# Spreading 512 token factors over all partitions: a store and a load in place of diagonals and a matmul, and the shift added one step later

## The chip, the cores and the metric

One core of a Trainium2 chip runs the kernel. The metric is the device time of one execution in microseconds; a comparison goes by the median of several executions. TensorE is called PE here (PEld its weight loads), VectorE DVE, ScalarE ACT, and SyncE SP, which issues every DMA of this kernel.

## The reference

One layer of a streaming encoder, 1024 tokens of width 2048, float32. A modulated RMSNorm is followed by one wide projection, two groups of heads, gates, an output projection, a residual and a last norm:

```
shift, scale, gate = split(silu(c) @ w_ada + b_ada, 3)
hn   = rmsnorm(x, norm_w) * (1 + scale) + shift          # the change is here
proj = hn @ w_in                                          # 2048 x 7184
a_out = differential attention (8 heads, rope, chunk mask), normed, gated
b_out = gated linear attention (4 heads, chunks of 64), normed, gated
out  = rmsnorm(x + gate * (concat(a_out, b_out) @ w_out), final_norm_w)
```

Per token t and channel k, hn[t,k] = x[t,k] * r[t] * a[k] + s[k], with r[t] the reciprocal root mean square of the token, a = norm_w * (1 + scale) and s = shift.

## The kernel before, in words

The tokens are worked in two halves of 512. In each half `hn` lies in SBUF transposed, as 16 tiles of 128 channels by 512 tokens. Every matrix is split into two parts, `hi` (rounded to the matmul's format) and `lo` (the rest), and each product is three matmuls, hi*hi, hi*lo, lo*hi. Weights come through `wload`: a DMA on SP into one of two `wr` buffers (L177), a rounding copy on ScalarE (L179), a subtraction on VectorE (L180), into one of three `w` buffers. `proj_b` (L190 to L192) and `proj_a` (L218 to L220) are the projections and fill most of PE's time.

A half goes through four groups g (`unit`), each with two attention heads and one head of gated linear attention. The attention of a head makes scores in one of two PSUM banks (`s`, L665, L666), takes their maximum on VectorE (L669, scaled at L673), the exponential on ScalarE (L678), then transposes (`tp`, L708) and multiplies with the values (`av`, L720 to L722). Small PSUM tiles of all stages (`tp`, `av`, the norms' sums, `o` and others) share the two banks of the pool `ms_p`.

`hn` of the second half is prepared while the first half runs, in small pieces of side work. The list `later` holds them, and `wload` takes one out after every second weight load (after two of three in the second half). The piece is traced behind ScalarE's rounding copy (`issue_after(paced.ins)`), which orders its ScalarE instructions alone; its VectorE instructions and DMAs have no such order. The tile framework's scheduler then lays out every engine's order from a timeline that it simulates, by priority in program order, and every engine and the DMA queue of SP work in that order. All side work goes through `stage`, two buffers of 128x512, which take turns:

- 16 pieces load x in token layout and square it with a sum on ScalarE (L932).
- `end` turns the sums into the 512 factors `r`, 128 partitions by 4 (`ssq[:, 20:24]`, L937 and `rsqrt_small`). They are needed along the free dimension on all partitions: four diagonals (L942), a matmul with ones into a bank of `ms_p` (L944), and a copy to `rb` (L945).
- 16 pieces load x transposed, multiply by `a_c` and `rb` (L949), add `s_c` (L950) and store the result in DRAM (`hn_d`, L951).

At the end of the first half, `second_hn` loads two channel tiles at a time back (`xtb`, L963) and splits them into the `hn` tiles as PE is done with the old ones: L229 (copy on ScalarE) and L230 (subtraction on VectorE), by the helper `split`. The first half does the same job by `activations`, with the shift added inside the split (L322, L323).

Behind the 16 pieces, `later` is filled with the rows of the adaLN gate (`gate_rows`, L918, L920, L912), 16 loads and multiply-adds per quarter; their accumulator `gacc` shares its buffer with `rb`.

Of the kernel before, what the change touches and what calls it, by code (L numbers as in the profile page):

```python
# [10 lines left out]
F32 = mybir.dt.float32  # L11
F32R = mybir.dt.float32r
BF16 = mybir.dt.bfloat16
AF = mybir.ActivationFunctionType
ALU = mybir.AluOpType
# [4 lines left out]
P = 128  # L20
# [3 lines left out]
TOK = 512  # L24
# [71 lines left out]
def body(ctx, tc, A, out):  # L96
    nc = tc.nc
    tc.keep_in_program_order(nc.scalar.preload_act_table_set("natural_log_exp_and_others"))
    V, G, SC, PE = nc.vector, nc.gpsimd, nc.scalar, nc.tensor
# [8 lines left out]
    misc = ctx.enter_context(tc.tile_pool(name="misc", bufs=1))  # L108
    pj_p = ctx.enter_context(tc.tile_pool(name="pj", bufs=4, space=PSUM))
    sc_p = ctx.enter_context(tc.tile_pool(name="sc", bufs=2, space=PSUM))  # L110
    ms_p = ctx.enter_context(tc.tile_pool(name="ms", bufs=2, space=PSUM))
    dram = ctx.enter_context(tc.tile_pool(name="dram", bufs=1, space=DRAM))
# [3 lines left out]
    vs_d = [dram.tile([P, 4, 2, P], F32, name=f"vsd{h}", tag=f"vsd{h}") for h in range(HEADS)]  # L116
    s_d = [dram.tile([P, 256], F32, name=f"sd{g}", tag=f"sd{g}") for g in range(GHEADS)]
    gate_d = dram.tile([1, D], F32, name="gate_d")
    hn_d = [dram.tile([P, 2, TOK], F32, name=f"hnd{k}", tag=f"hnd{k}") for k in range(KT // 2)]


    ident = const.tile([P, P], F32, name="ident")
# [3 lines left out]
    ones_f = ones.bitcast(F32)  # L126
# [11 lines left out]
    s_c = const.tile([P, KT], F32, name="s_c")  # L138
# [13 lines left out]
    def rsqrt_small(dst, src, n, scale):  # L152
        t = small()
        m = small()
        V.tensor_scalar(m[:, :n], src, scale, EPS, ALU.mult, ALU.add)
        SC.activation(t[:, :n], m[:, :n], AF.Ln)
        SC.activation(t[:, :n], t[:, :n], AF.Exp, scale=-0.5)
        V.tensor_mul(m[:, :n], m[:, :n], t[:, :n])
        V.tensor_mul(m[:, :n], m[:, :n], t[:, :n])
        V.tensor_scalar(m[:, :n], m[:, :n], -0.5, 1.5, ALU.mult, ALU.add)  # L160
        V.tensor_mul(dst, m[:, :n], t[:, :n])
# [25 lines left out]
    hn = [None] * KT  # L187
# [40 lines left out]
    def split(hi, lo, src, lo_eng=None):  # L228
        SC.copy(hi, src)  # L229
        (lo_eng or V).tensor_tensor(lo, src, hi.bitcast(F32), ALU.subtract)  # L230
# [36 lines left out]
    with tc.high_priority():  # L267
# [12 lines left out]
        m, r, t = rsb[:, 0, :], rsb[:, 1, :], acc_p.tile([P, TOK], F32, name="nt", tag="pt", bufs=6)  # L280
# [540 lines left out]
    def unit(half, g, first, kdec):  # L821
# [52 lines left out]
        if swap:  # L874
            second_hn()
# [52 lines left out]
    def norm_rows():  # L928
        ssq = const.tile([P, 24], F32, name="ssq_b")

        def sq(i, raw):
            SC.activation(raw, raw, AF.Square, accum_out=ssq[:, i:i + 1])  # L932
            if i == 15:
                end()

        def end():
            V.tensor_reduce(ssq[:, 16:20], ssq[:, 0:16].rearrange("p (t q) -> p t q", q=4), AX.X, ALU.add)  # L937
            rsqrt_small(ssq[:, 20:24], ssq[:, 16:20], 4, 1.0 / D)
            dg = misc.tile([P, 2, TOK], F32, name="rdiag", tag="rt", bufs=2)[:, 0, :]
            r_ = misc.tile([P, TOK], F32, name="rb", tag="gacc")  # L940
            for t_ in range(4):
                V.tensor_scalar(dg[:, t_ * P:(t_ + 1) * P], ident, ssq[:, 20 + t_:21 + t_], None, ALU.mult)  # L942
            ps_ = ms_p.tile([P, TOK], F32, name="rb_ps", tag="ms")
            PE.matmul(ps_, ones_f, dg, start=True, stop=True)  # L944
            SC.copy(r_, ps_)  # L945
            rb.append(r_)

        def act(kt, u):
            V.scalar_tensor_tensor(u, u, a_c[:, kt:kt + 1], rb[0], ALU.mult, ALU.mult)  # L949
            V.tensor_scalar_add(u, u, s_c[:, kt:kt + 1])  # L950
            nc.sync.dma_start(hn_d[kt // 2][:, kt % 2, :], u)  # L951

        x_row = lambda i: A["x"][TOK + i // 4 * P:TOK + (i // 4 + 1) * P, i % 4 * 512:(i % 4 + 1) * 512]
        return ([(x_row(i), lambda raw, i=i: sq(i, raw)) for i in range(16)]
                + [(A["xt"][1][:, kt, :], lambda u, kt=kt: act(kt, u)) for kt in range(KT)])

    def second_hn():
        while later:
            later.pop(0)()
        for k0 in range(0, KT, 2):  # L960
            tag = ("ka", "va", "kb")[k0 // 2 % 3]
            r3 = hd_p.tile([P, 2, TOK], F32, name=f"xtb{k0}", tag=tag, bufs=2 if tag == "kb" else None)
            nc.sync.dma_start(r3, hn_d[k0 // 2])  # L963
            for kk in range(2):
                kt = k0 + kk
                hn[kt] = hn_p.tile([P, 2, TOK], F32R, name=f"hn{kt}", tag=f"hn{kt}")
                split(hn[kt][:, 0, :], hn[kt][:, 1, :], r3[:, kk, :], lo_eng=V)


    later += run_ahead(norm_rows())  # L970
# [36 lines left out]
    for half in range(2):  # L1007
# [6 lines left out]
        ssq = const.tile([P, 4, N_SSQ], F32, name=f"ossq{half}", tag="ossq", bufs=2)  # L1014
        tot = const.tile([P, 8], F32, name=f"otot{half}", tag="otot", bufs=2)
        oview = out[half * TOK:(half + 1) * TOK, :].rearrange("(t p) c -> p t c", p=P)
        for m in range(4):
# [26 lines left out]
            for k0 in range(0, KT, 2):  # L1044
                w = wload(A["wout"][m][:, k0:k0 + 2, :], 1024)
                for t_ in range(4):
                    for kk in range(2):
                        kt = k0 + kk
# [59 lines left out]
```

## Time and profile before

| | us |
|---|---|
| median of 3 executions | 1954.24 (1954.07 to 1956.40) |
| the profiled execution, its own time | 1955.52 |
| its span, first to last instruction | 1953.7 |
| PE busy | 1905.5 |
| DVE busy | 1321.9 |
| ACT busy | 968.7 |

The profile is of one execution, so times read in it are set against its 1955.52 us; its span leaves 1.8 us around the instructions. Matmuls are pipelined, so the duration of one overlaps the next; the distance between two starts is what a matmul takes. In the stretch view, busy time that equals the length of the stretch means that PE had no gap. A wait is put down to what released it last.

### The profile page before, as it was taken

The page shows a single profiled execution, that of the slowest core. Times are in us where ns is not written, and L with a number is a line of the kernel's source. Part 1 is how long each engine was busy: PE and PEld are TensorE (multiplying, and loading weights), DVE is VectorE, ACT ScalarE, POOL GpSimd, SP SyncE. Part 2 cuts the span into 40 slices and gives each one's busy share as a digit, 9 for nine tenths or more (in the row PEclk, how much of TensorE's full clock was granted, in tenths as well). Part 3 has the DMA queues.
Part 4 walks back from the last instruction along what each step waited for, and adds up shares of the span by engine and source line. Part 5 has one row for each costly group of instructions (what it writes and reads, how often), then busy time and mean ns, then how long its engine had stood idle before and what let it go on. Part 6 is the DMA issues. An engine that isn't in the chain of part 4 may idle for free.

```text
span 1953.7 us, 28965 instructions
## 1 busy us (share of the span) xinstructions
PE 1905.5 (98%) x11118; PEld 1677.0 (86%) x11118; DVE 1321.9 (68%) x2496; ACT 968.7 (50%) x1811; POOL 0.7 (0%) x6
## 2 busy tenths in 40 slices
PE   7999999999989999999999999999999999899998
PEld 4888999899868989889899898989888998688888
DVE  7897876577779767656676666866785675534444
ACT  4222865566545566545545555554654544323323
POOL 0000000000000000000000000000000000000000
PEclk9899999999999999999999999999999999799999
DMA  9884434332665444433344323533263723466543
GB/s 362 294 290 136 155 125 141 119 106 87 209 210 166 136 138 150 135 89 101 97 154 117 106 91 108 162 111 99 87 198 117 267 86 106 167 239 213 162 150 120
DMA packets 111758, 298.16 MB, mean 153 GB/s; under 512 B 11098, under 2 KB 31322, under 8 KB 111108
## 3 DMA queue, kind: packets, MB, share of 16 engines
q1 hardware_dynamic: 111620, 296.32, 46.6%
q8 instruction: 87, 1.43, 0.3%
q14 instruction: 51, 0.42, 0.1%
HBM read 258.00 MB, written 38.28 MB: 152 GB/s over the span
## 4 chain that ended last, share of the span: by engine, by line
PE 86%; DMA 6%; DVE 6%; issue 1%; ACT 1%; SPq 0%; DVEq 0%; ACTq 0%
PE pa L218 8%; PE pa L220 8%; PE pa L219 8%; PE pa L1051 4%; PE pa L1052 4%; PE pa L1053 4%; PE pb_dk L190 2%; PE pb_dk L191 2%; PE pb_dk L192 2%; PE pb_gg L190 2%; PE pb_dg L191 2%; PE pb_dq L192 2%; PE pb_dq L191 2%; PE pb_dq L190 2%; PE pb_dg L192 2%; PE pb_gg L192 2%
## 5 line engine op out<-in xcount | busy, mean ns | idle before, releaser
L180 DVE TENSOR_TENSOR w<-wr,w 128x1024 fp32r<-128x1024 f32 (+1 forms) x294 | 352.1, 1198 | 276.0 <-ACT w L179 274.8
L179 ACT CAST w<-wr 128x1024 fp32r<-128x1024 f32 (+1 forms) x294 | 303.2, 1031 | 431.2 <-PE pa L1053 116.1
L220 PE MATMUL pa<-w,hn 128*128 128x256 f32 (+1 forms) x1152 | 328.2, 285 | 0.0
L218 PE MATMUL pa<-w,hn 128*128 128x256 f32 (+1 forms) x1152 | 327.7, 285 | 0.0
L219 PE MATMUL pa<-w,hn 128*128 128x256 f32 (+1 forms) x1152 | 327.7, 285 | 0.0
L219 PEld LDWEIGHTS pa<-w,hn 128*128 128x128 f32 x1152 | 219.6, 191 | 2.4 <-issue 0.2
L218 PEld LDWEIGHTS pa<-w,hn 128*128 128x128 f32 x1152 | 219.5, 191 | 2.3 <-issue 0.5
L220 PEld LDWEIGHTS pa<-w,hn 128*128 128x128 f32 x1152 | 219.5, 191 | 1.5 <-issue 0.2
L678 ACT ACTIVATE p<-s,sm 128x512 f32<-128x512 f32 (+2 forms) x192 | 110.7, 580 | 130.1 <-DVE sm L675 59.0
L1051 PE MATMUL pa<-w,mx 128*128 128x512 f32 x384 | 150.7, 392 | 0.4 <-DVE h L996 0.4
L1052 PE MATMUL pa<-w,mx 128*128 128x512 f32 x384 | 150.4, 392 | 0.0
L1053 PE MATMUL pa<-w,mx 128*128 128x512 f32 x384 | 149.9, 392 | 0.0
L669 DVE TENSOR_REDUCE sm<-s 128x1 f32<-128x512 f32 (+2 forms) x192 | 105.5, 551 | 46.7 <-PE s L666 44.1
L190 PE MATMUL pb_gg<-hn,w 128*128 128x512 f32 x224 | 88.1, 394 | 0.6 <-DVE vb L230 0.6
L191 PE MATMUL pb_dk<-hn,w 128*128 128x512 f32 x224 | 88.1, 393 | 0.0
L190 PE MATMUL pb_dk<-hn,w 128*128 128x512 f32 x224 | 88.1, 393 | 0.0
L190 PE MATMUL pb_dg<-hn,w 128*128 128x512 f32 x224 | 88.1, 393 | 0.0
L191 PE MATMUL pb_gg<-hn,w 128*128 128x512 f32 x224 | 88.0, 393 | 0.0
L192 PE MATMUL pb_dq<-hn,w 128*128 128x512 f32 x224 | 87.9, 392 | 0.0
L191 PE MATMUL pb_dg<-hn,w 128*128 128x512 f32 x224 | 87.8, 392 | 0.0
L192 PE MATMUL pb_gg<-hn,w 128*128 128x512 f32 x224 | 87.8, 392 | 0.0
L192 PE MATMUL pb_dk<-hn,w 128*128 128x512 f32 x224 | 87.6, 391 | 0.0
(394 smaller groups left out, 4376.9 us busy)
## 6 DMA issues: line engine op xcount, KB each, us to landing
wr<-in_winb SPq DMA_DIRECT2D x142, 512.0 KB, 3.8
wr<-in_wina SPq DMA_DIRECT2D x72, 512.0 KB, 3.8
wr<-in_wout SPq DMA_DIRECT2D x64, 512.0 KB, 3.5
ada<-in_wada SPq DMA_DIRECT2D x44, 512.0 KB, 5.0
stage<-in_wgate SPq DMA_DIRECT2D x64, 256.0 KB, 3.0
mx<-mixd SPq DMA_DIRECT2D x32, 512.0 KB, 8.1
ada_kdec<-in_wada SPq DMA_DIRECT2D x20, 512.0 KB, 6.6
mixd<-wr_d SPq DMA_DIRECT2D x16, 512.0 KB, 4.5
```

Source lines behind the costliest of these rows:

```text
L179: paced = SC.copy(w[:, 0, :n], raw[:, :n])
L180: (lo_eng or V).tensor_tensor(w[:, 1, :n], raw[:, :n], w[:, 0, :n].bitcast(F32), ALU.subtract)
L190: PE.matmul(ps, w_hi, h[:, 0, :], start=first, stop=False)
L191: PE.matmul(ps, w_hi, h[:, 1, :], start=False, stop=False)
L192: PE.matmul(ps, w_lo, h[:, 0, :], start=False, stop=last)
L218: PE.matmul(o, ah, wh, start=st, stop=False, skip_group_check=True)
L219: PE.matmul(o, ah, wl, start=False, stop=False, skip_group_check=True)
L220: PE.matmul(o, al, wh, start=False, stop=kt == KT - 1, skip_group_check=True)
L678: SC.activation(p_[:, :n], pss[pi][:, :n], AF.Exp, bias=nm, scale=0.125, accum_out=sm[:, 4 + 2 * m_ + pi:5 + 2 * m_ + pi])
L1051: PE.matmul(pss[t_], ah, wh, start=kt == 0, stop=False)
L1052: PE.matmul(pss[t_], ah, wl, start=False, stop=False)
L1053: PE.matmul(pss[t_], al, wh, start=False, stop=kt == KT - 1)
```

## The change

The factors go from SBUF to a DRAM row `r_d` by one DMA and from there to all 128 partitions by another. The diagonals, the matmul and the copy go. The 16 transposed rows no longer add the shift before they are stored; it is added when the two parts are made, the high part by an activation with a bias, the low part by one instruction with two scalar steps.

```
+    r_d = dram.tile([1, TOK], F32, name="r_d")
...
         def end():
             V.tensor_reduce(ssq[:, 16:20], ssq[:, 0:16].rearrange("p (t q) -> p t q", q=4), AX.X, ALU.add)
             rsqrt_small(ssq[:, 20:24], ssq[:, 16:20], 4, 1.0 / D)
-            dg = misc.tile([P, 2, TOK], F32, name="rdiag", tag="rt", bufs=2)[:, 0, :]
             r_ = misc.tile([P, TOK], F32, name="rb", tag="gacc")
-            for t_ in range(4):
-                V.tensor_scalar(dg[:, t_ * P:(t_ + 1) * P], ident, ssq[:, 20 + t_:21 + t_], None, ALU.mult)
-            ps_ = ms_p.tile([P, TOK], F32, name="rb_ps", tag="ms")
-            PE.matmul(ps_, ones_f, dg, start=True, stop=True)
-            SC.copy(r_, ps_)
+            nc.sync.dma_start(r_d.rearrange("o (t p) -> (o p) t", p=P), ssq[:, 20:24])
+            nc.sync.dma_start(r_, r_d[0:1, :].to_broadcast([P, TOK]))
             rb.append(r_)
 
         def act(kt, u):
             V.scalar_tensor_tensor(u, u, a_c[:, kt:kt + 1], rb[0], ALU.mult, ALU.mult)
-            V.tensor_scalar_add(u, u, s_c[:, kt:kt + 1])
             nc.sync.dma_start(hn_d[kt // 2][:, kt % 2, :], u)
...
                 hn[kt] = hn_p.tile([P, 2, TOK], F32R, name=f"hn{kt}", tag=f"hn{kt}")
-                split(hn[kt][:, 0, :], hn[kt][:, 1, :], r3[:, kk, :], lo_eng=V)
+                hi, lo, shift = hn[kt][:, 0, :], hn[kt][:, 1, :], s_c[:, kt:kt + 1]
+                SC.activation(hi, r3[:, kk, :], AF.Identity, bias=shift)
+                V.scalar_tensor_tensor(lo, r3[:, kk, :], shift, hi.bitcast(F32), ALU.add, ALU.subtract)
```

## Rows read from the trace of the kernel before

**Rows 1.** The page: busy us (share of the span) and instructions of each engine.

```profile
PE 1905.5 (98%) x11118; PEld 1677.0 (86%) x11118; DVE 1321.9 (68%) x2496; ACT 968.7 (50%) x1811; POOL 0.7 (0%) x6
```

**Rows 2.** Stretches: from:to, length, busy us per engine, clock, DMA share, GB/s.

```profile
506.00:545.00 39.00, 39.00 (x176) 32.34 (x175) 31.32 (x54) 21.02 (x38) 0.00 (x0) 1.00 0.69 227
545.00:575.00 30.00, 26.30 (x119) 19.95 (x117) 23.19 (x63) 13.09 (x29) 0.00 (x0) 1.00 0.67 209
575.00:610.00 35.00, 30.17 (x233) 28.49 (x232) 28.86 (x70) 18.10 (x38) 0.00 (x0) 1.00 0.63 194
...
759.00:784.00 25.00, 25.00 (x190) 24.08 (x189) 22.47 (x34) 15.75 (x26) 0.00 (x0) 1.00 0.53 173
```

**Rows 3.** Waits of PE, 545 to 610 us: total us, times, longest.

```profile
PE s L665 <- ACT p L678: 4.6, 5, 1.9
```

**Rows 4.** Waits of DVE, 545 to 610 us.

```profile
DVE stage L949 <- DMA stage<-in_xt: 6.8, 7, 3.1
DVE gacc L920 <- DMA stage<-in_wgate: 4.1, 5, 1.3
DVE gacc L918 <- DMA stage<-in_wgate: 1.8, 1, 1.8
```

**Rows 5.** Waits of DVE, 506 to 545 us.

```profile
DVE stage L949 <- DMA stage<-in_xt: 7.3, 4, 4.4
```

**Rows 6.** Timeline of PE around 504 us: start, us, instruction.

```profile
504.40 1.02 PE L944 MATMUL rb_ps<-rdiag,ones 128*128 128x512 f32 x2
...
505.49 0.39 PE L192 MATMUL pb_dk<-hn,w 128*128 128x512 f32 x1
```

**Rows 7.** Tile `ssq_b`: the instruction that finishes the factors.

```profile
L161 DVE TENSOR_TENSOR ssq_b<-sm,sm x1: 164/164/164, 462.1 to 462.1; 128x4 f32<-128x4 f32 x1
```

**Rows 8.** Tile `stage`: ns min/median/max, first and last start us.

```profile
L949 DVE SCALAR_TENSOR_TENSOR stage<-stage,a_c,rb x16: 744/752/755, 506.1 to 573.3; 128x512 f32<-128x512 f32 x16
L950 DVE TENSOR_SCALAR stage<-stage,s_c x16: 406/480/487, 508.0 to 574.6; 128x512 f32<-128x512 f32 x16
...
L918 DVE TENSOR_SCALAR gacc<-stage,vec x4: 475/483/486, 578.2 to 1415.5; 128x512 f32<-128x512 f32 x4
...
L912 DVE TENSOR_TENSOR gacc<-gacc,stage x4: 672/673/680, 617.4 to 1455.1; 1x512 f32<-1x512 f32 x4
```

**Rows 9.** The page: DMA issues, KB each, median us from issue to landing.

```profile
wr<-in_winb SPq DMA_DIRECT2D x142, 512.0 KB, 3.8
...
ind<-in_ind SPq DMA_DIRECT2D x1, 1.0 KB, 9.1
```

**Rows 10.** Line L951, the 16 stores of rows to DRAM.

```profile
DMA to landing us min/median/max: 2.0/2.5/5.0
```

**Rows 11.** Tile `gate_d`: its loads from one DRAM row to all partitions.

```profile
DMA to landing us min/median/max: 3.1/4.6/7.8
```

**Rows 12.** Tile `xtb`: the split of the second half.

```profile
L229 ACT CAST hn<-xtb x16: 602/616/620, 759.7 to 780.6; 128x512 fp32r<-128x512 f32 x16
L230 DVE TENSOR_TENSOR hn<-xtb,hn x16: 682/684/693, 760.4 to 782.9; 128x512 fp32r<-128x512 f32 x16
```

**Rows 13.** Line L322, the high part with bias in the first half.

```profile
L322 ACT ACTIVATE hn<-xt,s_c x16: 720/725/728, 25.8 to 174.2; 128x512 fp32r<-128x512 f32 x16
```

**Rows 14.** Line L323, the low part with the shift in the first half.

```profile
L323 DVE SCALAR_TENSOR_TENSOR hn<-xt,s_c,hn x16: 739/746/753, 26.7 to 176.5; 128x512 fp32r<-128x512 f32 x16
```

**Rows 15.** Timeline, 468 to 478 us: a weight load and a cast.

```profile
468.30 0.33 SPq L177 DMA_DIRECT2D wr<-in_wina  x1
...
477.55 1.05 ACT L179 CAST w<-wr 128x1024 fp32r<-128x1024 f32 x1 [1.73 <-PE pa L220]
```

**Rows 16.** Timeline, 779 to 791 us: the last split, the first users.

```profile
779.01 0.40 PE L190 MATMUL pb_dk<-hn,w 128*128 128x512 f32 x1
...
782.94 0.68 DVE L230 TENSOR_TENSOR hn<-xtb,hn 128x512 fp32r<-128x512 f32 x1
...
790.45 0.39 PE L192 MATMUL pb_dk<-hn,w 128*128 128x512 f32 x1
```

## The prediction

> **What bounds the kernel now.** I read the page first. PE is busy 1905.5 of 1953.7 us [rows 1], so a change pays only if it takes work off PE or fills one of PE's gaps, 48.2 us in all. The stretch view then shows where gaps stand near this change: none from 506 to 545 us (39.00 of 39.00), 3.70 us from 545 to 575 and 4.83 us from 575 to 610, 8.53 us together [rows 2]. The clock is 1.00 in all of them, so they are waits, not a slower PE. PE's waits in 545 to 610 name the cause: the largest is a score matmul (L665) waiting for ScalarE's exponential (L678), which frees its PSUM bank [rows 3]; that waits for VectorE's maximum. VectorE in turn stands, in the same stretch, 6.8 us for the x rows of the side work (L949) and 4.1 + 1.8 us for the gate rows that follow (L920, L918), 12.7 us in all [rows 4]. VectorE runs in order, so a side row whose load has not landed holds up the softmax behind it. PE loses 8.53 / 12.7 = 0.67 us for each us of such standing. But from 506 to 545, where PE has projections and the gated linear attention, VectorE stands 7.3 us for the same rows [rows 5] and PE loses nothing. The price of a side row thus depends on which stage it falls in.
>
> The last view is the time at which the factors come. They are finished on VectorE at 462.3 us (L161, 462.1 plus 0.16) [rows 7]. The matmul that spreads them runs only at 504.40 [rows 6], and the first of the 16 rows that use them at 506.1 [rows 8]. PE has no gap in between, the diagonals are made right behind L161, so what holds the matmul is its turn for one of the two banks of the `ms` pool, in which it stands in line with the heads' tiles. The 16 rows then run as fast as store, reload and arithmetic allow, 506.1 to 573.3, and the gate rows, which nothing paces on VectorE, follow from 578.2 to 617.4 [rows 8].
>
> **The change part by part.**
>
> *The matmul goes.* Between 504.40 and the start of L192 at 505.49 stand the two passes of the matmul and one L191 [rows 6]; L191 alone would take the 0.23 us by which such matmuls follow each other (48 of them, 779.01 to 790.45, with a few others between, give 0.24) [rows 16]. 1.09 - 0.23 = 0.86 us of a full PE come off. The four diagonals and the copy of `rb_ps` are on VectorE and ScalarE, in stretches where PE does not wait: nothing, and with that cover gone a bank and an `rt` buffer are free earlier, no loss.
>
> *Store and load.* Neither is in the trace. The store is 2 KB in 512 pieces of four bytes. Below, the fastest store of a row, 2.0 us; above, the `ind` load with its 128 pieces of eight bytes, 9.1 us, queued at the start of the kernel behind the first megabytes [rows 9, 10]. The load is like `gate_d` to all partitions: 3.1 to 7.8, median 4.6 [rows 11]. I take 2.5 (median of the row stores; the queue is light at 462 us) and 4.6, with two issues of 0.33 [rows 15]: the factors are in SBUF at 462.3 + 2.5 + 4.6 + 0.7 = 470.1. Bounds: 468.1 and 479.9. All of them lie before 506.1; the rows start 36 us earlier (26 to 38).
>
> *SP's queue.* The load waits on SP for the store. Behind it stand weight loads, the next at 468.30, whose cast runs at 477.55; with 3.8 us to land, 5.45 us are spare [rows 9, 15]. Holding SP from 462.6 to 465 costs nothing; even 9.1 us (to 472) use 3.7 of the 5.45.
>
> *VectorE's queue.* If the first row stands in VectorE's order before its factors have landed, the low parts of weights (L180) and attention's probabilities wait behind it, and PE for those. At most that is from about 463 to 479.9, 17 us; at least nothing. The planner simulates both DMAs too, so I take 1 us, at 0.67: +0.7.
>
> *The add goes from the rows.* 16 x 0.48 = 7.7 us of VectorE [rows 8]. Two buffers alternate, so the chain of rows loses 8 x 0.48 = 3.8 us. On PE it is nothing by itself: work that VectorE does while PE is full.
>
> *Side work moves.* The rows now end at 573.3 - 36.0 - 3.8 = 533.5, before the softmax stretch; the gate rows move from 578.2 to 538.4 and end at 577.6. So in 545 to 610 only the gate rows are left, in 32.6 us of it. They cost 4.83 us in 35 us [rows 2], 0.138 per us: 4.5. Of 8.53 us, 4.0 come back. Bounds: all 8.53 (the gate rows fall among projections, as the x rows did in 506 to 545), or none (a gate row costs there what both did).
>
> *Shift added at the split.* On ScalarE the cast of 0.616 us becomes an activation with bias, 0.725 as in the first half; on VectorE 0.684 becomes 0.746 [rows 12 to 14]: 16 x 0.11 = 1.7 us and 16 x 0.06 = 1.0 us. This is in 759 to 784, where PE is full and VectorE busy 22.47 of 25 us [rows 2]. The last low part starts at 782.94; its first user is among the last matmuls of `pb_dk`, which end around 790.45 [rows 16]. Even both amounts in a row, 2.7 us, leave some 4 us. Cost nothing; without that cover 2.7.
>
> Sum: -0.86 - 4.0 + 0.7 = -4.2 us. The profiled execution took 1955.52; 1951.3 for it. It was 1.28 above the median of the runs, so 1950.0 for the median. Bounds of the moved parts: -9.4 (1944.8) if every wait goes and VectorE never stands.
>
> **The rivals.** About 0.2% (3.9 us) is what a measurement here can tell from no change.
>
> Rival 1, the waits stay: the planner puts side rows into whatever gaps it sees on VectorE, and their loads land later than it assumes. For it: the gate rows alone made 4.83 us of gaps, and they now begin with the softmax stretch. Against it: the 7.3 us of standing in 506 to 545 cost PE nothing, and that is the kind of stretch to which the x rows move. Only the matmul is won, and up to 2 us: 1951.4 to 1953.4; with some new gap up to 1955.
>
> Rival 2, slower: VectorE stands for the factors at about 463. This takes the place of the wait for PSUM, which held up nobody. For it: VectorE is in order, and the attention of the group before still has tiles on it. With 17 us at 0.67 PE would lose 11.4 us: 1954.2 - 0.9 + 11.4 = 1964.7 if nothing else is won. It decides from (3.9 + 0.86) / 0.67 = 7.1 us of standing if no gap is filled, and from (3.9 + 4.9) / 0.67 = 13 us if 4.0 are. Against it: a planner that counts 5 us or more for the two DMAs places the rows behind them.
>
> Rival 3, slower too: the store is slow by its pieces. `ind` took 9.1 with 128 pieces [rows 9]; if all beyond the floor of 2.0 grew fourfold, the store would take 2.0 + 4 x 7.1 = 30.4 us. SP would be held until 492.7, the weight load due at 468.30 would come 24.4 late, less the 5.45 spare, less the two slabs in hand (one column of `pb_dk`, 11.4 us [rows 16]): PE starves 7.5 us, and the gain by the shift is gone, 1960.9. Against it: that 9.1 holds the wait behind the first loads, and may hold little else. The Trainium skill, "DMA: Bandwidth & Descriptors", section "Rules for kernel authors", speaks for this rival: a last dimension that is not contiguous becomes one descriptor per element. By that rule the time would be the 1960.9 of this rival, or less as the pieces cost less. No row before shows such a store.
>
> **How the numbers follow.** The shift with part of the gaps back, 0.52, its own range 1944.8 to 1953; four fifths of it are beyond 0.2%. Rival 1, 0.28, nearly all within 0.2%. Rival 2 with its smaller cousins, where a moved row costs a gap elsewhere, 0.15. Rival 3, 0.05. Faster by over 0.2%: 0.43; within: 0.38; slower: 0.19 (a little of the rivals 2 and 3 ends within). The forecast is the first case's sum, 1950.0. The range starts at 1944.8 and reaches into rival 2 to 1958.0, about 5.5 us lost less the matmul and a little more; some 0.05 lies below and 0.13 above.
>
> **What would show it.** Right: no L942, L944, L945 and L950; the first L949 near 470, the last near 534; the gate rows about 40 us earlier; gaps of PE in 545 to 610 down to 4 or 5 us and none new before; hn ready some 2 us later with PE full. Wrong: the first L949 still near 500 (something other than the bank held it, or rival 3), VectorE standing for `rb` for over 7 us (rival 2), or the same 8.5 us of gaps under another name (rival 1). A later stage that the planner lays out otherwise, with a different gap at its end, would also make the number wrong for a reason that this working does not hold.

## The result

The changed kernel takes 1969.17 us (median of four, 1964.03 to 1969.87) against 1954.93 for the one before, an estimated ratio of 1.0068 with a 95% interval of 1.0053 to 1.0082 (the two medians alone give 1.0073). The forecast was 1950.0 in 1944.8 to 1958.0, so the time lies 11 us above the range; 0.13 had been given to a time above it. The profiled execution took 1969.87 us, 14.35 more than the one before, and its span is 1968.1, longer by 14.4.

PE is busy 5.5 us longer than in [rows 1], the rest of the 14.4 us is standing:

```profile
PE 1911.0 (97%) x11116; PEld 1681.6 (85%) x11116; DVE 1316.7 (67%) x2476; ACT 967.8 (49%) x1810; POOL 0.7 (0%) x6
```

The stretch view of the changed kernel, columns as in [rows 2], with two stretches ahead of those shown there:

```profile
470.00:480.00 10.00, 9.65 (x76) 9.21 (x74) 3.63 (x10) 5.04 (x9) 0.00 (x0) 1.00 0.04 8
480.00:490.00 10.00, 3.03 (x14) 3.03 (x15) 5.55 (x10) 2.15 (x3) 0.00 (x0) 0.59 0.57 164
...
506.00:545.00 39.00, 38.62 (x186) 31.71 (x186) 27.68 (x45) 20.55 (x37) 0.00 (x0) 1.00 0.73 241
545.00:575.00 30.00, 26.64 (x112) 21.73 (x111) 22.45 (x57) 12.43 (x28) 0.00 (x0) 0.89 0.70 219
575.00:610.00 35.00, 30.67 (x190) 26.93 (x189) 28.67 (x71) 19.72 (x43) 0.00 (x0) 1.00 0.49 150
```

Two things are to be seen. From 480 to 490 PE works 3.03 of 10 us, in a place where it had no gap before, and DMA is all but idle just ahead of it (share 0.04). And the gaps of 545 to 610, of which 4.0 us were to come back, are still there: 3.36 + 4.33 = 7.69 us of 8.53.

The chain of work from 470 to 488 us says what PE waited for in the first (start, us, what):

```profile
470.23 8.73 DMA r_d<-ssq_b
478.98 5.45 DMA rb<-r_d
484.79 0.32 issue
485.11 0.75 DVE stage L946
...
486.97 1.01 PE kv L789 x3
```

The store of 2 KB takes 8.73 us, its load 5.45. The waits of VectorE and then of PE, 460 to 520 us (total, times, longest):

```profile
DVE stage L946 <- DMA rb<-r_d: 10.1, 1, 10.1
```

```profile
PE kv L789 <- DVE S L797: 7.3, 1, 7.3
```

VectorE's timeline shows the order that leads to it:

```profile
470.05 0.15 DVE L162 TENSOR_TENSOR ssq_b<-sm,sm 128x4 f32<-128x4 f32 x1
...
473.96 0.42 DVE L244 TENSOR_SCALAR gt<-gt 128x512 f32<-128x512 f32 x1
484.45 1.41 DVE L946 SCALAR_TENSOR_TENSOR stage<-stage,a_c,rb 128x512 f32<-128x512 f32 x2 [10.06 <-DMA rb<-r_d]
486.44 0.47 DVE L797 SCALAR_TENSOR_TENSOR S<-S,decay,kv 128x256 f32<-128x256 f32 x1
```

The factors are finished at 470.2 (L162, the L161 of before). The first row that uses them (L946) stands 4.2 us of work behind that in VectorE's order, and the two DMAs take 14.2. VectorE works in order, so it stands for 10.06 us, and the state update of the gated linear attention (L797), which needs nothing of the factors, waits behind the first two rows. PE runs dry 5 us after VectorE did and stands 7.32.

PE's timeline behind that gap, matmuls of 256 columns:

```profile
489.69 0.41 PE L219 MATMUL pa<-w,hn 128*128 128x256 f32 x1
489.91 0.41 PE L220 MATMUL pa<-w,hn 128*128 128x256 f32 x1
...
492.42 0.28 PE L221 MATMUL pa<-w,hn 128*128 128x256 f32 x1
492.54 0.28 PE L219 MATMUL pa<-w,hn 128*128 128x256 f32 x1
```

They follow each other by 0.22 us, and from 492 on by 0.12. The granted clock is 0.50 in the stretches 486.97 to 489.5 and 489.5 to 491.5, which is the lower level, 1.2 GHz, after 7.32 us in which PE had stood. Some 4.6 us of work at half speed cost 2.3 us more.

The other changed steps, by tile: first the rows and gate rows (`stage`, as [rows 8]), then the split (`xtb`, as [rows 12]):

```profile
L946 DVE SCALAR_TENSOR_TENSOR stage<-stage,a_c,rb x16: 745/751/755, 484.4 to 550.6; 128x512 f32<-128x512 f32 x16
...
L919 DVE TENSOR_SCALAR gacc<-stage,vec x4: 476/478/485, 553.7 to 1427.4; 128x512 f32<-128x512 f32 x4
...
L913 DVE TENSOR_TENSOR gacc<-gacc,stage x4: 672/676/680, 595.1 to 1466.1; 1x512 f32<-1x512 f32 x4
```

```profile
L964 ACT ACTIVATE hn<-xtb,s_c x16: 707/716/724, 772.0 to 793.2; 128x512 fp32r<-128x512 f32 x16
L965 DVE SCALAR_TENSOR_TENSOR hn<-xtb,s_c,hn x16: 741/746/752, 772.8 to 795.3; 128x512 fp32r<-128x512 f32 x16
```

**The account.** The first split starts 12.3 us later than in [rows 12] (772.0 against 759.7). Of that, 2.1 us lie before the change begins: the first matmul of `proj_a` starts at 212.2 against 210.1, and executions differ there by about as much. The other 10.2 us are the gap, 7.32; the lower clock behind it, 2.3; the matmul that went, -0.86; gaps from 506 to 610, 8.07 instead of 8.53, -0.46; and a second spell of the lower clock, from about 554 to 561 us behind two gaps of 1.83 and 1.52, some 3 us (clock 0.93 over 550 to 600, where before shows 1.00). That makes 11.3, one more than measured. The last 2 us come behind the split: in 1650 to 1700 us PE has 0.9 us more of gaps, and the granted clock is 0.76 where before shows 0.80, which over 39 us of work is some 1.6 us by estimate. That is the place; no run shows why the change should reach it.

### The profile page after: what moved, and what is told of

Read it like the earlier page. It is cut to its first block, busy times and chain, and to the rows that moved or that the text cites. A ratio compares the mean times of both kernels' runs of the same rounds, so it can differ in the third digit from the quotient of the medians.

```text
span 1968.1 us, 28940 instructions
## 1 busy us (share of the span) xinstructions
PE 1911.0 (97%) x11116; PEld 1681.6 (85%) x11116; DVE 1316.7 (67%) x2476; ACT 967.8 (49%) x1810; POOL 0.7 (0%) x6
## 2 busy tenths in 40 slices
DMA packets 112430, 298.43 MB, mean 152 GB/s; under 512 B 11642, under 2 KB 31866, under 8 KB 111780
## 4 chain that ended last, share of the span: by engine, by line
PE 83%; DMA 8%; DVE 6%; ACT 1%; issue 1%; SPq 0%; DVEq 0%; ACTq 0%
PE pa L219 8%; PE pa L221 8%; PE pa L220 8%; PE pa L1049 4%; PE pa L1050 4%; PE pa L1051 4%; PE pb_gg L191 2%; PE pb_gg L192 2%; PE pb_gg L193 2%; PE pb_dk L192 2%; PE pb_dk L191 2%; PE pb_dk L193 2%; PE pb_dq L193 2%; PE pb_dq L192 2%; PE pb_dq L191 2%; PE pb_dg L192 2%
```

## The experiments

The stretch that differs is small, so the kernels are compared by three things: the time, the standing of VectorE for the load of `rb` (a dash where `rb` still comes from the matmul), and PE's gaps. Standing and gaps are those of one profiled execution of each. The kernel before takes 1955.2 to 1955.9 in these comparisons.

| kernel | us | ratio to before (95%) | VectorE stands for `rb` | gap of PE at 480 | gaps of PE, 506 to 610 |
|---|---|---|---|---|---|
| changed | 1969.17 | 1.0068 (1.0053 to 1.0082) | 10.06 | 7.32 | 8.07 |
| shift alone | 1956.85 | 1.0010 (1.0001 to 1.0019) | - | 0 | 8.47 |
| store and load alone | 1964.89 | 1.0047 (1.0032 to 1.0062) | 10.3 | 7.55 | 5.65 |
| changed, store in 128 pieces | 1958.31 | 1.0013 (1.0003 to 1.0022) | 1.5 | 0 | 7.67 |
| changed, rows later | 1956.14 | 1.0005 (0.9996 to 1.0014) | 0 | 0 | 7.55 |
| before, with an unused store and load | 1953.38 | 0.9992 (0.9983 to 1.0002) | - | 0 | 7.75 |
| changed, side work paced on VectorE | 1953.75 | 0.9995 (0.9985 to 1.0005) | 10.3 | 7.53 | 0 |
| 128 pieces and paced | 1944.26 | 0.9945 (0.9930 to 0.9959) | 1.7 | 0 | 0 |
| before, paced | 1949.03 | 0.9965 (0.9952 to 0.9978) | - | 0 | 3.13 |
| shift alone, paced | 1949.28 | 0.9967 (0.9956 to 0.9977) | - | 0 | 3.37 |

My theory was that the store is slow by its pieces of four bytes and VectorE stands for it; the rivals were that the shift at the split, or SP held by the store, costs the time.

**Each part alone.** The shift moved, diagonals and matmul kept (shown against the changed kernel):

```
+            dg = misc.tile([P, 2, TOK], F32, name="rdiag", tag="rt", bufs=2)[:, 0, :]
...
+            for t_ in range(4):
+                V.tensor_scalar(dg[:, t_ * P:(t_ + 1) * P], ident, ssq[:, 20 + t_:21 + t_], None, ALU.mult)
+            ps_ = ms_p.tile([P, TOK], F32, name="rb_ps", tag="ms")
+            PE.matmul(ps_, ones_f, dg, start=True, stop=True)
+            SC.copy(r_, ps_)
-            nc.sync.dma_start(r_d.rearrange("o (t p) -> (o p) t", p=P), ssq[:, 20:24])
-            nc.sync.dma_start(r_, r_d[0:1, :].to_broadcast([P, TOK]))
```

> The factors still go by diagonals and matmul; only the shift moves into the split. Theory (the loss comes from VectorE standing about 10 us for the factors' load): no wait for `rb` by DMA, no PE gap between 470 and 500 us, time within 1950 to 1957, ratio 0.998 to 1.001. Rival (the longer split, or the order that the planner makes without the adds, carries the loss): 1962 or more, with the gap near 760 to 800 us or in other places.

It gains nothing, and its 0.1% is within what can't be told from no change. The rows run from 510.1 to 570.8, and PE's gaps add up to those of before (8.47 against 8.53), though they lie in other places. The granted clock is below 1.00 here too, as in the changed kernel (in a profiled execution of 1959.77, 2.9 above the median):

```profile
545.00:575.00 30.00, 24.37 (x102) 19.50 (x100) 21.16 (x54) 10.44 (x25) 0.00 (x0) 0.89 0.71 231
```

Then the store and load alone, with the shift still added to the rows:

```
+            V.tensor_scalar_add(u, u, s_c[:, kt:kt + 1])
...
-                SC.activation(hi, r3[:, kk, :], AF.Identity, bias=shift)
-                V.scalar_tensor_tensor(lo, r3[:, kk, :], shift, hi.bitcast(F32), ALU.add, ALU.subtract)
+                split(hn[kt][:, 0, :], hn[kt][:, 1, :], r3[:, kk, :], lo_eng=V)
```

> The factors go by store and load; the add stays with the rows. Theory: VectorE stands 8 to 11 us for `rb`, PE has a gap of 6 to 8 us around 480 us and a lower granted clock behind it, 1963 to 1970. Rival (the split or the missing adds carry the loss): 1952 to 1957 although VectorE stands.

The store takes 8.8 us, VectorE stands 10.3, PE 7.55, and most of the loss is there (+9.0 of 14.2 us). So the gap at 480 lies with the two DMAs and not with the shift. The two parts alone come to 10.0 us, though, and the other 4 us come only with both. The traces show them in 506 to 610: the changed kernel has 2.4 us more of gaps there and the spell of lower clock of some 3 us, where store and load alone show 1.00 throughout. Why the two together make them wasn't tested.

**The store in other pieces.** Partition p holds tokens 4p to 4p+3, so that its four factors are one piece of 16 bytes:

```
-            nc.sync.dma_start(r_d.rearrange("o (t p) -> (o p) t", p=P), ssq[:, 20:24])
+            nc.sync.dma_start(r_d.rearrange("o (p t) -> (o p) t", p=P), ssq[:, 20:24])
...
-        x_row = lambda i: A["x"][TOK + i // 4 * P:TOK + (i // 4 + 1) * P, i % 4 * 512:(i % 4 + 1) * 512]
+        x_tok = A["x"][TOK:2 * TOK, :].rearrange("(p t) c -> t p c", t=4)
+        x_row = lambda i: x_tok[i // 4][:, i % 4 * 512:(i % 4 + 1) * 512]
```

> As after, but the 16 token rows are dealt out so that a partition's four factors are neighbours: the store is 128 pieces of 16 bytes instead of 512 of 4. If the 8.7 us of the store come from its number of pieces: 2.0 to 4.5 us, VectorE stands 4 to 6 us instead of 10, PE's gap there 0 to 3 us, 1955 to 1961. If they are a latency that does not depend on pieces: 8 to 9 us again and 1964 to 1970.

Store and load of that kernel (tile `r_d`; the load is issued when the store has landed), and VectorE's wait for it:

```profile
L941 SPq DMA_DIRECT2D r_d<-ssq_b x1: 326/326/326, 468.3 to 468.3; - x1
L942 SPq DMA_DIRECT2D rb<-r_d x1: 326/326/326, 469.7 to 469.7; - x1
```

```profile
DVE stage L946 <- DMA rb<-r_d: 1.5, 1, 1.5
```

The store takes 1.4 us, the gap at 480 is gone, and the time falls by 10.9 us. This is the kernel that the prediction had in mind: factors there at about 474, rows from 474.0 to 539.0. Yet it gains nothing on before. (The profiled execution took 1954.18, 4.1 below the median of ten; what the slower ones lose is not in its trace.) Its timeline of PE and VectorE shows why:

```profile
539.01 0.75 DVE L946 SCALAR_TENSOR_TENSOR stage<-stage,a_c,rb 128x512 f32<-128x512 f32 x1 [3.10 <-DMA stage<-in_xt]
...
540.86 0.39 PE L666 MATMUL s<-kb,qt 128*128 128x256 f32 x1 [2.04 <-ACT p L679]
...
542.22 0.48 DVE L919 TENSOR_SCALAR gacc<-stage,vec 128x512 f32<-128x512 f32 x1 [1.50 <-DMA stage<-in_wgate]
...
543.39 0.58 PE L666 MATMUL s<-kb,qt 128*128 128x256 f32 x1 [1.56 <-ACT p L679]
```

The next group's score matmuls come earlier here too, 540.86 where before has this one:

```profile
547.22 0.39 PE L665 MATMUL s<-kb,qt 128*128 128x256 f32 x1 [0.27 <-ACT p L678]
```

The last row and the first gate rows again stand in front of their maxima: 4.28 us of gaps in 506 to 545, where there had been none, and 3.39 in 545 to 610. That the earlier side work is what moved these matmuls isn't shown: in the next kernel the rows start later than in before, and the same matmul comes at 532.17.

**The slow store kept, its user later.** Eight empty pieces ahead of the rows, and the first two rows ordered on VectorE behind the weight's subtraction:

```
+    side = {}
...
-            (lo_eng or V).tensor_tensor(w[:, 1, :n], raw[:, :n], w[:, 0, :n].bitcast(F32), ALU.subtract)
+            side["low"] = (lo_eng or V).tensor_tensor(w[:, 1, :n], raw[:, :n], w[:, 0, :n].bitcast(F32), ALU.subtract)
...
+            if kt < 2:
+                with tc.issue_after(side["low"].ins):
+                    V.scalar_tensor_tensor(u, u, a_c[:, kt:kt + 1], rb[0], ALU.mult, ALU.mult)
...
-    later += run_ahead(norm_rows())
+    side_work = run_ahead(norm_rows())
+    later += side_work[:17] + [lambda: None] * 8 + side_work[17:]
```

> As after, with the slow store of 512 pieces, but eight empty pieces stand ahead of the 16 transposed rows, and the first two rows' VectorE instruction is ordered behind the weight subtraction of its weight load: VectorE first needs the factors some 30 us later than in after. SP still stands behind the store. Theory (VectorE's standing is the loss, SP's is not): no standing for `rb`, no gap around 480 us, 1951 to 1957. Rival (SP held 8.7 us by the store starves the weights): a gap between 475 and 510 us stays, 1960 or more.

The store still takes 8.6 us and holds SP (469.1 to 477.8), but no row stands for it (first row 514.4) and PE has no gap from 465 to 500:

```profile
470.00:480.00 10.00, 10.00 (x84) 9.91 (x83) 9.24 (x19) 6.45 (x10) 0.00 (x0) 1.00 0.03 0
480.00:490.00 10.00, 10.00 (x86) 10.00 (x85) 6.80 (x10) 3.75 (x7) 0.00 (x0) 1.00 0.66 186
```

The time is 1956.14, no change from before. So the store's duration costs nothing by itself; VectorE's standing does.

**SP alone held.** The kernel before, with the store and a load that writes to an unread half of a buffer:

```
+    r_d = dram.tile([1, TOK], F32, name="r_d")
...
-            dg = misc.tile([P, 2, TOK], F32, name="rdiag", tag="rt", bufs=2)[:, 0, :]
+            dg2 = misc.tile([P, 2, TOK], F32, name="rdiag", tag="rt", bufs=2)
+            dg = dg2[:, 0, :]
+            nc.sync.dma_start(r_d.rearrange("o (t p) -> (o p) t", p=P), ssq[:, 20:24])
+            nc.sync.dma_start(dg2[:, 1, :], r_d[0:1, :].to_broadcast([P, TOK]))
```

> The kernel before, diagonals and matmul and all, with the store and the load added to a spare plane that nobody reads: only SP's queue and the DMA engines feel them. Theory (SP's spare time covers the store): 1954 to 1958, no gap around 480 us. Rival (the queue of SP alone costs): 1960 or more.

SP is held 9.6 us, from the store to the load that waits for it, and the time doesn't grow:

```profile
L942 SPq DMA_DIRECT2D r_d<-ssq_b x1: 377/377/377, 463.4 to 463.4; - x1
L943 SPq DMA_DIRECT2D rdiag<-r_d x1: 326/326/326, 473.0 to 473.0; - x1
```

Weight loads had room for that.

**Pacing.** The front of this document says that a piece of side work is ordered behind ScalarE's rounding copy on ScalarE alone. Here its VectorE instructions are ordered too, behind the weight's subtraction:

```
-            (lo_eng or V).tensor_tensor(w[:, 1, :n], raw[:, :n], w[:, 0, :n].bitcast(F32), ALU.subtract)
+            low = (lo_eng or V).tensor_tensor(w[:, 1, :n], raw[:, :n], w[:, 0, :n].bitcast(F32), ALU.subtract)
...
-                with tc.issue_after(paced.ins):
+                with tc.issue_after(paced.ins), tc.issue_after(low.ins):
```

> As after, but the VectorE part of each piece of side work is also ordered behind the weight subtraction of its own weight load, so a row comes every second weight load (about 12 us) and its load has long landed. Theory (the loss, and the gaps of the kernel before in 545 to 610 us, are both VectorE standing for side loads in order): no standing for `rb`, no PE gaps between 470 and 610 us, 1943 to 1950. Rival (the gaps come with the softmax whatever the rows do): gaps of 5 us or more stay in 545 to 610 us and the time is 1951 to 1957.

PE's wait at 480, which had been expected to go, stays, with VectorE standing 10.3 for `rb`:

```profile
PE kv L789 <- DVE S L797: 7.5, 1, 7.5
```

But all gaps from 506 to 610 are gone, since the rows now come one by one until 613.7 and the gate rows far behind them, and the time is 15.4 us below the changed kernel. With both edits:

> The store of 128 pieces and the pacing of VectorE's side rows together. Theory (two separate stands of VectorE, for the factors and for the side rows, each with its own gap): no gap between 470 and 610 us, 1943 to 1950, faster than both kernels. Rival (a gap that is closed comes back at the next stage): 1952 to 1957.

The stretch view of that kernel:

```profile
506.00:545.00 39.00, 39.00 (x181) 32.48 (x181) 33.10 (x71) 24.51 (x50) 0.00 (x0) 1.00 0.67 212
545.00:575.00 30.00, 30.00 (x153) 25.36 (x152) 21.52 (x58) 19.23 (x41) 0.00 (x0) 1.00 0.45 144
575.00:610.00 35.00, 35.00 (x262) 33.45 (x261) 26.55 (x52) 17.41 (x32) 0.00 (x0) 1.00 0.43 131
```

PE is full, and 1944.26 us beat both kernels, by 11 and 25 us. Against the paced kernel with the slow store it gains 9.5 us, which is the price of the gap at 480 and the lower clock behind it (7.32 + 2.3 in the changed kernel) measured a second way. To see what of it is the change, the same pacing in the kernel before, and in the one with the shift alone:

> The kernel before with the pacing of VectorE's side rows alone. Theory: the 8.5 us of gaps between 545 and 610 us go, nothing stands in their place, 1944 to 1951. Rival (the gaps are the softmax's own): 1952 to 1957 with gaps of 5 us or more there.

> Diagonals and matmul as before, the shift added in the split, and the side rows paced on VectorE. It parts what is left between the paced kernel before (1949.0 us) and the paced one with the 128-piece store (1944.3 us). If the transfer by store and load is worth it (0.9 us of PE and an earlier bank): 1948 to 1950 here. If the shift's move is worth it (one add and a later store less per row): 1944 to 1946. If both: about 1947.

Pacing alone is worth 0.35%. In the paced kernel before, rows still start only at 508.9 and end at 611.1, 6.8 us apart where the kernel with both edits has 8.6 (474.3 to 603.4). VectorE still stands for their loads in 506 to 610, and a wait of the kind of [rows 3] is left:

```profile
DVE stage L949 <- DMA stage<-in_xt: 9.9, 7, 4.6
...
PE s L665 <- ACT p L678: 3.1, 3, 1.3
```

Moving the shift adds nothing to that (1949.28). The other 4.8 to 5.0 us down to 1944.26 come with the factors at 474 instead of 507 to 509: 0.86 for the matmul by the prediction's estimate, 3.1 to 3.4 for these gaps, about one that I can't place.

**What makes the store slow.** Two kernels measure stores by themselves. Each is the kernel before with five more stores of the same factors, each loaded back, one after the other on SP, so that their own times (1985.56 and 1961.09 us) say nothing. `dst` holds the forms of the table below: those of its first four lines and the last were in the first kernel, those 64 bytes apart, and those with two times again, in the second. The loop is that of the second; the first differs in where the stores of one factor begin.

```
+            cur = ssq[:, 20:24]
+            for i in range(5):
...
+                nc.sync.dma_start(dst[i], view(cur if i < 3 else cur[:, 0:1]))
+                nc.sync.dma_start(view(nxt), dst[i])
+                cur = nxt
```

> A measurement inside the kernel before: five stores of the factors, each with its load back, one behind the other on SP, in this order: 512 pieces of 4 bytes whose neighbours in DRAM come from different partitions (as in after); 128 of 16 bytes; 512 of 4 bytes, neighbours from one partition with a gap of 4 bytes; 256 of 8 bytes; 128 of 4 bytes. From issue to the issue of its load: if the number of pieces sets the time, 8 to 9, about 1.5 to 2.5, 8 to 9, about 4, about 1.5 to 2.5 us. If the size of a piece does: the 128 of 4 bytes take 8 to 9. If neighbours from different partitions do: the first alone takes 8 to 9, the third 2 to 3.

> A measurement in the kernel before: it keeps the diagonals and adds five stores of factors to five more DRAM tiles, each with its load back, one after the other on SP, so its own time says nothing. Read is the time from a store's issue to the issue of its load, which waits for the store. The stores: 512 pieces of 4 bytes that lie 64 bytes apart in DRAM; 128 pieces of 16 bytes without gaps; 128 pieces of 16 bytes that start 64 bytes apart; 128 pieces of 4 bytes that start 64 bytes apart; 128 pieces of 4 bytes without gaps. Theory that a piece of 4 bytes is slow wherever it lies: about 6 to 9 us for the first, fourth and fifth, 1.4 for the second and third. Theory that pieces are slow where several fall into the same 64 bytes of DRAM: the first and fourth and third fall to 1.4 to 2.5, the second is 1.4 to 2, the fifth stays at 8.

SP's timeline of the first, two of its five stores (L952) with the load that waits for each (L953), and a weight load (L178):

```profile
467.41 0.38 SPq L952 DMA_DIRECT2D md<-ssq_b  x1
476.61 0.38 SPq L953 DMA_DIRECT2D rdiag<-md  x1
...
500.07 0.33 SPq L952 DMA_DIRECT2D md<-rdiag  x1
500.45 0.43 SPq L178 DMA_DIRECT2D wr<-in_winb  x1
508.24 0.32 SPq L953 DMA_DIRECT2D rdiag<-md  x1
```

And of the second:

```profile
463.36 0.38 SPq L952 DMA_DIRECT2D md<-ssq_b  x1
466.14 0.38 SPq L953 DMA_DIRECT2D rdiag<-md  x1
467.99 0.33 SPq L952 DMA_DIRECT2D md<-rdiag  x1
...
469.40 0.32 SPq L953 DMA_DIRECT2D rdiag<-md  x1
...
476.88 0.32 SPq L952 DMA_DIRECT2D md<-rdiag  x1
478.36 0.32 SPq L953 DMA_DIRECT2D rdiag<-md  x1
479.90 0.32 SPq L952 DMA_DIRECT2D md<-rdiag  x1
480.26 1.51 SPq L178 DMA_DIRECT2D wr<-in_winb  x1
488.64 0.32 SPq L953 DMA_DIRECT2D rdiag<-md  x1
```

The times from a store's issue to its load's, from both kernels, with the share in which the DMA engines were busy in that time:

| store | pieces in one 64 bytes of DRAM | us | DMA share |
|---|---|---|---|
| 512 of 4 bytes, as in the change | 16, from 16 partitions | 9.20 | 0.03 |
| 128 of 4 bytes, no gaps | 16, from 16 partitions | 8.17 and 8.74 | 0.96 and 0.76 |
| 512 of 4 bytes, 8 bytes apart | 8, from 2 partitions | 6.03 | 0.04 |
| 256 of 8 bytes, no gaps | 8, from 8 partitions | 3.18 | 0.05 |
| 512 of 4 bytes, 64 bytes apart | 1 | 2.78 | 0.10 |
| 128 of 16 bytes, 64 bytes apart | 1 | 1.87 | 0.04 |
| 128 of 4 bytes, 64 bytes apart | 1 | 1.48 | 0.05 |
| 128 of 16 bytes, no gaps | 4, from 4 partitions | 1.42 and 1.41 | 0.06 and 0.06 |

The theory that a piece of four bytes is slow wherever it lies falls with the two stores 64 bytes apart. The stores of 512 pieces of four bytes settle the rest: the same number and size takes 9.20, 6.03 or 2.78 us, as 16, 8 or one of them lie in the same 64 bytes of DRAM. So what costs here is that pieces of four bytes lie close together. The 128 pieces without gaps don't add to that: both times a weight load was issued right behind the store and was under way with it, and no run has such a store alone, so its 8.17 and 8.74 us may be those of the traffic. Other distances than 64 bytes were not tried, so how long the stretch is that they must not share stays open, and so does why 256 pieces of 8 bytes do better than 512 of 4.

## Why the prediction was wrong, step by step

**The step that failed first: VectorE's queue, +0.7.** It took 1 us of standing, and 10.06 came. It rested on two numbers. The store was taken as 2.5 us by the row stores of [rows 10], and was 8.73; the bound above, 9.1 by `ind`, held. And the planner was trusted to place the first row behind both DMAs; it left 4.2 us for 14.2. The same step's price per us of standing came out near, 7.32 / 10.06 = 0.73 where 0.67 was taken, but by luck: a standing of 10.06 cost PE 7.32, two of 10.3 cost 7.55 and 7.53, and those of 1.5 and 1.7 cost nothing, which is a slack of some 2.7 us and then the whole, and not a share of each. Left out was the clock: the gap is followed by 2.3 us of loss at the lower level. With 9.6 us for the term instead of 0.7, the sum would have been +4.7; the next step holds the larger part of what is then missing.

Rival 2 named this, with its place and its threshold (7.1 us of standing), and gave 1964.7; it had 0.15 together with its cousins. That a bound of my own (the store at 9.1) led straight past that threshold should have raised it.

**The second: side work moves, -4.0.** Of 8.53 us, 0.84 came back in 545 to 610 and 0.38 new ones came in 506 to 545, and the lower clock behind two of them cost some 3 us more: about +2.5 where -4.0 was said. That isn't the late start alone: with the quick store the rows ended at 539.0, near the 533.5 of the forecast, and the gaps were 7.67. The rows of before showed standing in 506 to 545 for nothing [rows 5], and I took that for a property of the time. It was one of the work that then lay there: in the kernel with the quick store two score matmuls that before has from 547.22 on stand at 540.86 and 543.39, and the standing fell on them again. What put them there is open, as they came earlier still in the kernel with late rows, whose gaps were 7.55. That the waits stay is what Rival 1 said, and for the quick store it is the result (1.0013). The paced kernels show that these gaps are ended by spreading the side work over VectorE's time, not by starting it earlier.

**What held.** The matmul's 0.86 us: nothing contradicts it, but it is too small to be seen alone. SP's hold is free: shown by the kernel before with the unused store (9.6 us of hold, 0.9992) and by the late rows. The shift at the split costs nothing: 0.716 and 0.746 us a piece where 0.725 and 0.746 were said, PE 26.00 of 26 us busy in 771 to 797; the shift alone is within 0.2%. Beside the slow store the shift's move goes with 4.3 us more (1969.17 against 1964.89), in 506 to 610 and not at the split. Rival 3 was right that the store is slow, more by how its pieces lie than by how many they are, and wrong in where it hurts: SP could wait, VectorE could not. The rule of the Trainium skill that stood there ("DMA: Bandwidth & Descriptors", section "Rules for kernel authors": a last dimension that is not contiguous becomes one descriptor per element) agrees with the page of the profile: packets under 512 bytes are 11642 in the changed kernel and 11258 with pieces of 16 bytes, 384 = 512 - 128 fewer. The price does not go by that count, as 9.20 and 2.78 us for 512 pieces each show.

**Open.** The factors are finished at 470.2 us in the changed kernel and at 468.4 with both edits, against 462.3 before, 463.4 with the unused store and 466.4 with the shift alone. Of the last, 4.0 us are a later start (its first matmul of `proj_a` comes at 214.1), and 2.1 us of the first; the rest there is another order on VectorE, whose reason I didn't test. The 4 us that come only with both parts, and the 2 us behind the split, have a place and no cause shown. That the matmul of before waited for a bank is a reading too: PE runs without a gap up to it, and no run parts the bank from the planned order.

## What to carry to other kernels

When a matmul that spreads a small vector is replaced by two DMAs, ask first who stands behind the first user on its in-order engine, and order that user late by hand: here the DMAs' 14 us cost nothing with the user later, and nearly 10 us of PE with it early. Store such a vector so that each partition writes one piece of 16 bytes, not 4-byte pieces that interleave. And gaps that come from side work in front of a critical instruction are removed by pacing the side work on the engine that both share; only then was the earlier start worth its 5 us.

## What the runs showed of the hardware

The store of 512 interleaved pieces of four bytes took 8.6 to 9.6 us with the DMA engines nearly idle (share 0.03 to 0.04), the same pieces each in its own 64 bytes of DRAM took 2.78, and the same bytes in 128 pieces of 16 took 1.4. The load back of the 2 KB to all partitions took 5.45 us in the changed kernel, within the 3.1 to 7.8 of [rows 11]. And a gap of 7.32 us of PE was followed by 4.6 us at a granted clock of 0.50, the 1.2 GHz level, which put almost a third on top of its price.
